# A decoder trunk on one core: the second MLP's down projection as seven block products in place of eight

## The chip, the core and the metric

The kernel runs on one core of one Trainium2 chip. The core has five engines that run side by side, each with its own queue in a fixed order: TensorE (PE; matrix products into PSUM), VectorE (DVE), ScalarE (ACT), GpSimd (POOL) and the queues that issue transfers (SP among them). The metric is the device time of one execution in microseconds, the median of several runs.

## What is computed

The reference is a decoder trunk of two layers on 1024 tokens of width 1024, all in fp32. The first layer mixes the tokens with a state-space recurrence, the second with stick-breaking attention. Each ends with a squared-ReLU MLP of inner width 4096:

```
h = modulate(rms_norm(x, mlp_norm_g[i]), sh_m, sc_m)
ff = einsum('bsf,fd->bsd', square(relu(einsum('bsd,df->bsf', h, mlp_w1[i]))), mlp_w2[i])
x = x + g_m[:, None, :] * ff
```

The change is in the second layer's `mlp_w2` product, 4096 x 1024 by 1024 tokens.

## The kernel before

Activations lie with features on the 128 partitions and tokens along the row, in tiles of 128 x 512: `xs[k][h]` is feature tile k (of 8) and token half h (of 2). Each fp32 product is made of three matmuls (`mm3`, lines 242 to 248): the weight and the activation are each split into a rounded upper part (written by ScalarE, type fp32r) and the rest (a subtraction on VectorE), and upper x upper, upper x lower and lower x upper are added in PSUM. A weight unit is 128 x 1024, eight blocks of 128 x 128; `load_unit` (line 205) fetches it into `raw`, and `split_unit` makes `uh` and `ul` of it. There are three buffers each of raw, uh and ul.

`mlp` (line 856) goes through the 32 inner tiles in eight groups of four. `up` makes one inner tile for one token half: 24 matmuls into a `pm` accumulator (two of these), relu on ScalarE, a square on VectorE (line 77), and the split of the result into two `f` tiles (ScalarE line 875, VectorE line 83). `down` takes the four inner tiles of a group to one output tile and token half: 12 matmuls into a `pa` accumulator (six of these), and one VectorE instruction, the gain (line 92): x = pa * mod + x. Group c's down part stands after the first up unit of group c + 1, so that TensorE has work while the last inner tiles are finished; then the other three up units of c + 1 follow. One w2 unit serves two output tiles; four make a group. The last group is different: its down part runs by token halves, and each finished tile is written out.

Outside the stretches that `keep_in_program_order` pins, a scheduler in the compiler sets the order of each queue; the MLP is such code. A tile's buffer is used again in turn, and the instruction that writes it next waits for all users of the old contents.

In the second MLP the norm's tiles (`acc`, `sq`, `rr`, `nt`) lie in a pool `np2` of their own, and `r` has two buffers, `f` 24.

## Time and profile before

| what | before |
|---|---|
| median of 3 runs | 2548.94 us (2546.42 to 2551.44) |
| the profiled execution | 2540.94 us, span 2539.2 us |
| TensorE busy | 2385.0 us, 94% of the span, 12704 matmuls |
| VectorE / ScalarE / GpSimd busy | 61% / 36% / 28% |
| mean granted TensorE clock | 0.975 of full speed |

The span is the time from the first to the last instruction; what lies around it is 1.7 us. In the profile a busy share over the whole span is a mean over stages: the second MLP fills roughly the last 700 us, and there GpSimd does nothing at all after its start. Matmuls overlap one another, so the listed time of one is longer than the distance from one to the next.

### The profile page before, as it was taken

What the parts mean: (1) busy time and instruction counts of PE and PEld (TensorE: products, weight loads), DVE (VectorE), ACT (ScalarE), POOL (GpSimd) and SP (SyncE); (2) the same over time, 40 slices, a digit from 0 to 9 for tenths busy, and PEclk for the clock granted to TensorE, in tenths of its full rate; (3) what the DMA queues carried; (4) which work ended last, traced back from release to release, by engine and by line L of the source; (5) the groups of instructions that cost most, each with busy time, mean ns of one, the idle gap of its engine ahead of it and who ended that gap; (6) DMA issues with size and microseconds to landing.
All of it is one profiled execution on the core that took longest, in us unless ns stands there. A gap on an engine that the chain in (4) does not pass through costs nothing.

```text
span 2539.2 us, 32956 instructions
## 1 busy us (share of the span) xinstructions
PE 2385.0 (94%) x12704; PEld 2009.2 (79%) x12704; DVE 1551.4 (61%) x2284; ACT 909.4 (36%) x1644; POOL 709.3 (28%) x795
## 2 busy tenths in 40 slices
PE   3888999999899999999899999999999999999999
PEld 2677788878687888888788888877788888888887
DVE  7997547776566553356777778788663333333334
ACT  4653124221121122133566666666341122112211
POOL 4664460385786000023333333332200000000000
PEclk8898999999999999999999999999999999999999
DMA  4325862767667441132111111246621111111112
GB/s 148 87 76 197 286 213 96 240 226 244 224 216 261 147 141 50 43 121 95 53 69 66 56 35 63 80 138 203 222 75 50 50 50 43 49 50 50 50 50 100
DMA packets 105918, 299.17 MB, mean 118 GB/s; under 512 B 13344, under 2 KB 25632, under 8 KB 105760
## 3 DMA queue, kind: packets, MB, share of 16 engines
q1 hardware_dynamic: 87840, 242.52, 28.1%
q0 software_dynamic: 15360, 50.34, 5.5%
q10 hardware_dynamic: 2560, 4.20, 0.7%
q8 instruction: 100, 1.64, 0.3%
q14 instruction: 58, 0.48, 0.1%
HBM read 243.33 MB, written 49.48 MB: 115 GB/s over the span
## 4 chain that ended last, share of the span: by engine, by line
PE 65%; DVE 15%; DMA 10%; issue 4%; ACT 2%; POOL 1%; SPq 0%; DVEq 0%; ACTq 0%; POOLq 0%
PE pm L69 8%; PE pm L246 8%; PE pm L247 8%; PE pm L248 8%; PE pa L248 6%; PE pa L246 6%; PE pa L247 6%; DMA raw<-in_adaT_dram 6%; PE pt L69 3%; DVE junk L173 3%; DVE sn L1114 3%; PE z L69 2%; PE po L69 2%; DMA raw<-in_wT_dram 1%; PE pv L246 1%
## 5 line engine op out<-in xcount | busy, mean ns | idle before, releaser
L246 PE MATMUL pm<-h,uh 128*128 128x512 f32 x1200 | 467.6, 392 | 7.6 <-ACT r L872 7.6
L248 PE MATMUL pm<-h,ul 128*128 128x512 f32 x1200 | 469.0, 391 | 4.5 <-DVE ul L83 4.4
L247 PE MATMUL pm<-h,uh 128*128 128x512 f32 x1200 | 468.8, 391 | 0.5 <-DVE h L92 0.5
L213 ACT CAST uh<-raw 128x1024 fp32r<-128x1024 f32 x162 | 170.4, 1052 | 741.9 <-PE pa L247 382.9
L246 PE MATMUL pa<-f,uh 128*128 128x512 f32 x848 | 332.1, 392 | 5.9 <-DVE xall L92 2.9
L247 PE MATMUL pa<-f,uh 128*128 128x512 f32 x848 | 331.7, 391 | 0.2 <-DVE f L83 0.2
L248 PE MATMUL pa<-f,ul 128*128 128x512 f32 x848 | 331.5, 391 | 0.0
L83 DVE TENSOR_TENSOR ul<-raw,uh 128x1024 fp32r<-128x1024 f32 x162 | 206.9, 1277 | 183.0 <-ACT uh L213 178.1
L246 PEld LDWEIGHTS pm<-h,uh 128*128 128x128 f32 x1200 | 225.9, 188 | 57.6 <-ACT r L872 10.6
L248 PEld LDWEIGHTS pm<-h,ul 128*128 128x128 f32 x1200 | 226.0, 188 | 52.7 <-DVE ul L83 5.8
L247 PEld LDWEIGHTS pm<-h,uh 128*128 128x128 f32 x1200 | 226.1, 188 | 47.5 <-DVE h L92 1.1
L92 DVE SCALAR_TENSOR_TENSOR x<-pa,mod,x 128x512 f32<-128x512 f32 x143 | 106.5, 750 | 204.6 <-PE pa L248 200.1
L173 DVE CUSTOM_DVE_ANT_0 junk<-raw,silr 128x1024 bf16<-128x1024 f32 x95 | 137.3, 1446 | 151.9 <-DMA raw<-in_adaT_dram 151.8
L69 PE MATMUL pm<-uh,h 128*128 128x256 f32 x960 | 225.4, 301 | 4.1 <-POOL h L74 3.0
L1114 DVE TENSOR_TENSOR_SCAN sn<-sn 128x768 f32<-128x768 f32 (+7 forms) x128 | 180.2, 1414 | 47.6 <-ACT sn L1109 46.3
L246 PEld LDWEIGHTS pa<-f,uh 128*128 128x128 f32 x848 | 160.0, 189 | 40.2 <-DVE xall L92 3.8
L247 PEld LDWEIGHTS pa<-f,uh 128*128 128x128 f32 x848 | 160.1, 189 | 33.7 <-DVE f L83 0.5
L248 PEld LDWEIGHTS pa<-f,ul 128*128 128x128 f32 x848 | 160.1, 189 | 33.2
L69 PEld LDWEIGHTS pm<-uh,h 128*128 128x128 f32 x960 | 170.3, 198 | 6.2 <-POOL h L74 3.2
L875 ACT CAST f<-r 128x512 fp32r<-128x512 f32 x128 | 79.5, 621 | 240.5 <-DVE r L77 240.5
L80 POOL TENSOR_TENSOR acc<-acc,sq 128x512 f32<-128x512 f32 x36 | 51.6, 1433 | 384.7 <-ACT sq L816 364.6
L77 DVE TENSOR_TENSOR r<-r 128x512 f32<-128x512 f32 (+1 forms) x130 | 97.5, 750 | 95.9 <-ACT r L872 95.9
(345 smaller groups left out, 4458.9 us busy)
## 6 DMA issues: line engine op xcount, KB each, us to landing
raw<-in_w_dram SPq DMA_DIRECT2D x144, 512.0 KB, 3.3
raw<-in_adaT_dram SPq DMA_DIRECT2D x96, 512.0 KB, 4.2
uh<-kh SPq DMA_DIRECT2D x40, 512.0 KB, 4.1
ul<-kl SPq DMA_DIRECT2D x40, 512.0 KB, 4.1
kh<-kr POOLq DMA_DIRECT2D x64, 256.0 KB, 2.6
kl<-ks POOLq DMA_DIRECT2D x64, 256.0 KB, 3.7
raw<-in_wT_dram SPq DMA_DIRECT2D x24, 512.0 KB, 4.2
raw<-in_wglu_dram SPq DMA_DIRECT2D x20, 512.0 KB, 4.4
```

Source lines behind the costliest of these rows:

```text
L69: return lambda *a, **k: tc.keep_in_program_order(f(*a, **k))
L77: eng.tensor_tensor(o, a, b, op=ALU.mult)
L80: eng.tensor_tensor(o, a, b, op=ALU.add)
L83: eng.tensor_tensor(o, a, b, op=ALU.subtract)
L92: V.scalar_tensor_tensor(o, a, s, b, op0=op0, op1=op1)
L173: V.tensor_tensor_reduce(junk, raw, row, 1.0, 0.0, op0=ALU.mult, op1=ALU.add, accum_out=bcol)
L213: ACT.copy(uh, raw)
L246: T.matmul(ps, uh[:, sl], hi, start=first, stop=False)
L247: T.matmul(ps, uh[:, sl], lo, start=False, stop=False)
L248: T.matmul(ps, ul[:, sl], hi, start=False, stop=last)
L875: ACT.copy(hi, r)
L1114: V.tensor_tensor_scan(g[:, s0:], g[:, s0:], g[:, s0:], 1.0, op0=ALU.mult, op1=ALU.bypass)
```

## The change

For groups 1 to 6 of the second MLP the down projection of one w2 unit is taken as a 2 x 2 block product. The left blocks are the weights: the two output tiles of the unit (i) by the inner tiles 0, 1 and 2, 3 (A11, A12, A21, A22, each two 128 x 128 blocks). The right blocks are the activations: the inner tiles 0, 1 and 2, 3 by the two token halves (B11, B12, B21, B22). Eight block products become seven, of block sums (Winograd's form): `RIGHT` says which right factor each takes. Products are 6 matmuls each, so an output pair is 42 in place of 48.

What that needs: per group, `enter` makes four sums of two tiles each (T1 to T4; eight VectorE instructions) and splits seven right blocks in place of four (14 tiles in place of 8). Per w2 unit, `blocks` copies the upper part of A11, A12 and A22 on ScalarE (768 wide) and makes the lower part on VectorE; then GpSimd makes four sums of 256 columns within raw and splits the result itself (a 1024-wide cast and a 1024-wide subtraction) into a second uh and ul. So a unit takes two of the three uh and ul buffers. Per output pair, the seven products end in seven gains and four adds on VectorE and one copy on ScalarE; the partial sums u and v are in the two `t` tiles, and three of the gains read those in place of PSUM.

Buffers in the second MLP: `r` six in place of two, `f` 30 in place of 24 (shared with the norm's tiles, which were in np2), `t` two, raw two in place of three. The pool is opened ahead of the output projection. w2's blocks are laid out in another order on the host (`W2_COLS`). Groups 0 and 7, and the first MLP, keep the plain form; in the last group two splits are made later (`plain`).

```diff
...
 LEAD = 24
+W2_COLS = (range(8), (0, 1, 2, 3, 6, 7, 4, 5))
...
     def open_x(i):
         es = ExitStack()
         pools["x"] = es.enter_context(tc.tile_pool(name=f"xp{i}", bufs=16 if i else 1))
-        pools["raw"] = es.enter_context(tc.tile_pool(name=f"raw{i}", bufs=3))
+        pools["raw"] = es.enter_context(tc.tile_pool(name=f"raw{i}", bufs=3 - i))
         es.callback(pools.pop, "raw")
         turns.clear()
         return es
...
             self.pool = (1, 3, 5, 7)
 
         def tile(self, tag, bufs):
+            if callable(self.np_):
+                return self.np_(tag, bufs)
             return self.np_.tile([P, HN], F32, tag=tag, name=nm(tag), bufs=bufs)
 
         def square(self, k, h):
...
                     stt(lo, t, shift, hi, ALU.add, ALU.subtract)
 
 
-    def mlp(layer, xs, hs, norm, mid=None, done=None):
+    def open_f(n):
+        fp = ctx_f.enter_context(tc.tile_pool(name="fp", bufs=1))
+
+        def ft(tag, bufs, dt=F32):
+            return fp.tile([P, HN], dt, tag=tag, name=nm(tag), bufs=bufs)
+
+        def f_tile(dt=F32R):
+            return ft("f", n, dt)
+
+        return ft, f_tile
+
+    def mlp(layer, xs, hs, norm, fs, mid=None, done=None):
         w1, w2 = A["w1"][layer], A["w2"][layer]
         gm = M_GM0 if layer == 0 else M_GM1
-        es = ExitStack()
-        fp = es.enter_context(tc.tile_pool(name="fp", bufs=1))
-
-        def ft(tag, bufs, dt=F32):
-            return fp.tile([P, HN], dt, tag=tag, name=nm(tag), bufs=bufs)
-
-        hid = {}
+        ft, f_tile = fs
+        hid, raws = {}, {}
 
         def up(f, u, h):
             p = ps_mm()
             for k in range(8):
                 mm3(p, u, k, hs[k][h], k == 0, k == 7)
-            r = ft("r", 2)
+            r = ft("r", 2 + 4 * layer)
             ACT.activation(r, p, AF.Relu)
             mul(r, r, r)
-            hi, lo = ft("f", 20 + 4 * layer, F32R), ft("f", 20 + 4 * layer, F32R)
+            return r
+
+        def halves(r):
+            hi, lo = f_tile(), f_tile()
             ACT.copy(hi, r)
             sub(lo, r, hi)
-            hid[f, h] = (hi, lo)
-
-        def down(c, o, u, j0, h):
+            return hi, lo
+
+        def down(c, o, u, i, h):
             p = ps_ax()
             for j in range(4):
-                mm3(p, u, j0 + j, hid[4 * c + j, h], j == 0, j == 3)
+                mm3(p, u, W2_COLS[layer][4 * i + j], hid[j, h], j == 0, j == 3)
             stt(xs[o][h], p, mod[:, gm + o:gm + o + 1], xs[o][h], ALU.mult, ALU.add)
+
+
+        def enter(j, h, r):
+            raws[j, h] = r
+            if h == 0 and j < 2:
+                hid["B11", j] = halves(r)
+            if (j, h) == (1, 1):
+                for i in range(2):
+                    t = ft("t", 2)
+                    sub(t, raws[i, 1], raws[i, 0])
+                    hid["T1", i] = halves(t)
+            if h == 1 and j >= 2:
+                i = j - 2
+                b11, b12, b21, b22 = raws[i, 0], raws[i, 1], raws[j, 0], raws[j, 1]
+                hid["B21", i] = halves(b21)
+                hid["B22", i] = halves(b22)
+                sub(b12, b22, b12)
+                hid["T3", i] = halves(b12)
+                add(b11, b11, b12)
+                hid["T2", i] = halves(b11)
+                sub(b21, b21, b11)
+                hid["T4", i] = halves(b21)
+
+        def blocks(c, op):
+            raw = raw_tile()
+            SP.dma_start(raw, w2[c, op])
+            h0, l0, h1, l1 = un_tile("uh"), un_tile("ul"), un_tile("uh"), un_tile("ul")
+            ACT.copy(h0[:, 0:768], raw[:, 0:768])
+            sub(l0[:, 0:768], raw[:, 0:768], h0[:, 0:768])
+            a11, a12, a22, a21 = [raw[:, 256 * n:256 * n + 256] for n in range(4)]
+            add(a22, a21, a22, G)
+            sub(a21, a11, a21, G)
+            sub(a11, a22, a11, G)
+            sub(a12, a12, a11, G)
+            G.tensor_copy(h1, raw)
+            sub(l1, raw, h1, G)
+            return {**{k: (h0, l0, 256 * n) for n, k in enumerate((1, 2, 4))},
+                    **{k: (h1, l1, 256 * n) for n, k in enumerate((6, 3, 5, 7))}}
+
+        RIGHT = {1: "B11", 2: "B21", 3: "B22", 4: "T4", 5: "T1", 6: "T2", 7: "T3"}
+
+        def seven(c):
+            us, sums, op_ = {}, {}, [0]
+
+            def gain(i, h, src):
+                k = 2 * op_[0] + i
+                stt(xs[k][h], src, mod[:, gm + k:gm + k + 1], xs[k][h], ALU.mult, ALU.add)
+
+            def product(op, n):
+                if op not in us:
+                    us[op] = blocks(c, op)
+                uh, ul, o = us[op][n]
+                p = ps_ax()
+                for i in range(2):
+                    hi, lo = hid[RIGHT[n], i]
+                    sl = slice(o + 128 * i, o + 128 * i + 128)
+                    T.matmul(p, uh[:, sl], hi, start=(i == 0), stop=False)
+                    T.matmul(p, uh[:, sl], lo, start=False, stop=False)
+                    T.matmul(p, ul[:, sl], hi, start=False, stop=(i == 1))
+                op_[0] = op
+                if n == 1:
+                    sums[op] = ft("t", 2), ft("t", 2)
+                    ACT.copy(sums[op][0], p)
+                if n < 3:
+                    gain(0, 0, p)
+                elif n == 4:
+                    gain(1, 0, p)
+                elif n == 6:
+                    add(sums[op][0], p, sums[op][0])
+                elif n == 5:
+                    u, v = sums[op]
+                    add(v, p, u)
+                    gain(0, 1, v)
+                elif n == 7:
+                    u, v = sums[op]
+                    add(u, p, u)
+                    gain(1, 0, u)
+                    add(v, p, v)
+                    gain(1, 1, v)
+                else:
+                    gain(0, 1, p)
+
+            for op in range(4):
+                for n in (1, 2, 4, 6, 5, 7, 3):
+                    product(op, n)
+
+        def plain(c, j, h, r):
+            raws[j, h] = r
+            late = c == 7 and layer == 1
+            if not late or h == 0 or j > 1:
+                hid[j, h] = halves(r)
+            elif j == 1:
+                hid[0, 1], hid[1, 1] = halves(raws[0, 1]), halves(r)
+
+        def fast(c):
+            return layer == 1 and 0 < c < 7
+
+        def ups(c, j):
+            u = load_unit(w1[4 * c + j])
+            for h in range(2):
+                r = up(4 * c + j, u, h)
+                if fast(c):
+                    enter(j, h, r)
+                else:
+                    plain(c, j, h, r)
 
         for h in range(2):
             for f in range(4):
                 u = load_unit(w1[f])
-                up(f, u, h)
+                plain(0, f, h, up(f, u, h))
                 if h == 0 and f == 0:
                     norm.rstd(1)
                 elif h == 0 and f == 1:
...
                     norm.apply(1, 0, 8)
         for c in range(8):
             if c < 7:
-                u = load_unit(w1[4 * c + 4])
-                up(4 * c + 4, u, 0)
-                up(4 * c + 4, u, 1)
-                for op in range(4):
-                    u = load_unit(w2[c, op])
-                    for i in range(2):
-                        for h in range(2):
-                            down(c, 2 * op + i, u, 4 * i, h)
-                    if mid is not None:
-                        mid()
-                for f in range(4 * c + 5, 4 * c + 8):
-                    u = load_unit(w1[f])
-                    up(f, u, 0)
-                    up(f, u, 1)
+                held = dict(hid)
+                hid.clear()
+                ups(c + 1, 0)
+                nxt = dict(hid)
+                hid.clear()
+                hid.update(held)
+                if fast(c):
+                    seven(c)
+                else:
+                    for op in range(4):
+                        u = load_unit(w2[c, op])
+                        for i in range(2):
+                            for h in range(2):
+                                down(c, 2 * op + i, u, i, h)
+                        if mid is not None:
+                            mid()
+                hid.clear()
+                hid.update(nxt)
+                for j in range(1, 4):
+                    ups(c + 1, j)
                     if mid is not None:
                         mid()
             else:
...
                     for op in range(4):
                         u = load_unit(w2[c, op])
                         for i in range(2):
-                            down(c, 2 * op + i, u, 4 * i, h)
+                            down(c, 2 * op + i, u, i, h)
                             done(2 * op + i, h)
-        es.close()
 
 
     def attention(xn, bias, xd):
...
         cyc[0] += 1
         pump((3, 4)[cyc[0] % 2])
 
-    mlp(0, xs, hs, norm=norm, mid=mid, done=done0)
+    ctx_f = ExitStack()
+    mlp(0, xs, hs, norm, open_f(20), mid=mid, done=done0)
+    ctx_f.close()
     norm1.rstd(1)
     norm1.spread(1)
     norm1.pool = (1, 4)
...
         for k in range(8):
             xs2[k][h] = xt()
             SP.dma_start(xs2[k][h], xd[k][h])
-    norm2.np_ = ctx.enter_context(tc.tile_pool(name="np2", bufs=1))
+    ctx_f = ctx
+    fs = open_f(30)
+    spare = {}
+
+    def norm_tile(tag, bufs):
+        n = spare.setdefault(tag, [0, []])
+        n[0] += 1
+        if len(n[1]) < bufs:
+            n[1].append(fs[1](F32))
+        return n[1][(n[0] - 1) % bufs]
+
+    norm2.np_ = norm_tile
 
     def oproj(i, h, mms):
         p = ps_mm() if (i, h) == (NONE, 1) else ps_ax()
...
     def done1(k, h):
         SP.dma_start(out[k][:, HN * h:HN * h + HN], xs2[k][h])
 
-    mlp(1, xs2, hs2, norm=norm2, done=done1)
+    mlp(1, xs2, hs2, norm2, fs, done=done1)
 
 
 def _constants(np):
...
     a["wo"] = unit(sb_w_o[0])
     a["wT"] = np.concatenate([w_kv.T, sb_w_q[0].T], 0).reshape(24, 128, 1024)
     a["w1"] = np.stack([unit(w) for w in mlp_w1])
-    a["w2"] = np.stack([w.reshape(8, 4, 128, 4, 2, 128).transpose(0, 3, 2, 4, 1, 5).reshape(8, 4, 128, 1024)
-                        for w in mlp_w2])
+    a["w2"] = np.stack([w.reshape(8, 4, 128, 4, 2, 128).transpose(0, 3, 2, 4, 1, 5).reshape(8, 4, 128, 8, 128)[
+        :, :, :, list(cols)].reshape(8, 4, 128, 1024) for w, cols in zip(mlp_w2, W2_COLS)])
     return {k: np.ascontiguousarray(v) for k, v in a.items()}
```

The queues differ as follows. On VectorE, a w2 unit within a group before: the second unit's split, then a gain for each output tile and token half, then the next unit's split (x are the output tiles, pa the accumulators).

```order
L83 TENSOR_TENSOR ul_18484<-raw_18481,uh_18483 128x1024
L92 SCALAR_TENSOR_TENSOR x_16428<-pa_18363,mod,x_16428 128x512
L92 SCALAR_TENSOR_TENSOR x_16444<-pa_18377,mod,x_16444 128x512
L92 SCALAR_TENSOR_TENSOR x_16430<-pa_18391,mod,x_16430 128x512
L92 SCALAR_TENSOR_TENSOR x_16446<-pa_18405,mod,x_16446 128x512
L83 TENSOR_TENSOR ul_18546<-raw_18543,uh_18545 128x1024
```

After, in the same place: the gains of one output pair, with the adds into u and v (t) between them, and behind them the short split (768 wide) for the unit of the pair after the next.

```order
L93 SCALAR_TENSOR_TENSOR x_16428<-pa_20345,mod,x_16428 128x512
L93 SCALAR_TENSOR_TENSOR x_16428<-pa_20356,mod,x_16428 128x512
L93 SCALAR_TENSOR_TENSOR x_16430<-pa_20364,mod,x_16430 128x512
L81 TENSOR_TENSOR t_20352<-pa_20372,t_20352 128x512
L81 TENSOR_TENSOR t_20353<-pa_20380,t_20352 128x512
L93 SCALAR_TENSOR_TENSOR x_16444<-t_20353,mod,x_16444 128x512
L81 TENSOR_TENSOR t_20352<-pa_20389,t_20352 128x512
L81 TENSOR_TENSOR t_20353<-pa_20389,t_20353 128x512
L93 SCALAR_TENSOR_TENSOR x_16444<-pa_20400,mod,x_16444 128x512
L93 SCALAR_TENSOR_TENSOR x_16430<-t_20352,mod,x_16430 128x512
L93 SCALAR_TENSOR_TENSOR x_16446<-t_20353,mod,x_16446 128x512
L84 TENSOR_TENSOR ul_20488<-raw_20485,uh_20487 128x768
```

So four instructions between two splits have become eleven; three of the gains take t as their input, and the short split stands behind all of them.

On TensorE before, the last product of one accumulator's chain and the beginning of the next; each chain of 12 is closed before the next begins.

```order
L248 MATMUL pa_18363<-f_18119,ul_18360 128x512
L246 MATMUL pa_18363<-f_18189,uh_18359 128x512
L247 MATMUL pa_18363<-f_18190,uh_18359 128x512
L248 MATMUL pa_18363<-f_18189,ul_18360 128x512
L246 MATMUL pa_18377<-f_17763,uh_18359 128x512
L247 MATMUL pa_18377<-f_17764,uh_18359 128x512
```

After, the end of the third product of a pair (from the first half-unit, uh_20333 and ul_20334) and what follows it, from GpSimd's half-unit (uh_20335 and ul_20336).

```order
L954 MATMUL pa_20364<-f_20184,ul_20334 128x512
L952 MATMUL pa_20372<-f_20094,uh_20335 128x512
L953 MATMUL pa_20372<-f_20095,uh_20335 128x512
L952 MATMUL pa_20380<-f_20008,uh_20335 128x512
L953 MATMUL pa_20380<-f_20009,uh_20335 128x512
L952 MATMUL pa_20389<-f_20089,uh_20335 128x512
L953 MATMUL pa_20389<-f_20090,uh_20335 128x512
L954 MATMUL pa_20372<-f_20094,ul_20336 128x512
L952 MATMUL pa_20372<-f_20179,uh_20335 128x512
L953 MATMUL pa_20372<-f_20180,uh_20335 128x512
L954 MATMUL pa_20372<-f_20179,ul_20336 128x512
L954 MATMUL pa_20380<-f_20008,ul_20336 128x512
```

The products 6, 5 and 7 are begun with their upper weights, two matmuls each, and only then does the first one come that needs GpSimd's lower part: 24 matmuls into the pair, where the upper part is needed after 18. Where a group's first pair stands, the products are not interleaved.

## Rows read from the trace of the kernel before

**Rows 1.** Busy time by stretch: time, busy us and count of each engine, clock, DMA.
```profile
core 0: us, PE busy (x) PEld busy (x) DVE busy (x) ACT busy (x) POOL busy (x), PEclk, DMA share, GB/s
420.00:800.00 380.00, 362.26 (x1576) 295.95 (x1574) 260.15 (x313) 83.19 (x117) 238.30 (x271) 0.98 0.66 227
1800.00:1850.00 50.00, 46.50 (x216) 37.48 (x215) 35.13 (x60) 22.34 (x33) 17.05 (x12) 1.00 0.51 192
1850.00:1900.00 50.00, 49.05 (x216) 40.29 (x215) 32.57 (x45) 22.49 (x33) 0.00 (x0) 1.00 0.28 92
1900.00:2500.00 600.00, 600.00 (x2648) 497.12 (x2647) 225.16 (x277) 121.95 (x164) 0.00 (x0) 1.00 0.15 50
```

**Rows 2.** The chain of waits from 1700 us to the end, by line.
```profile
by line: PE pa L248 14.3%; PE pa L246 14.2%; PE pa L247 14.2%; PE pm L246 13.7%; PE pm L247 13.7%; PE pm L248 13.7%; PE pm L69 3.7%; PE po L69 1.3%; PE z L69 1.1%; PE pt L69 1.0%; issue 0.9%; DMA ro<-od 0.9%; DMA ul<-kl 0.8%; DMA od<-o 0.8%
```

**Rows 3.** TensorE's waits from 1840 us to the end: total, times, longest.
```profile
PE pm L246 <- ACT r L872: 1.0, 1, 1.0
```

**Rows 4.** VectorE's timeline, second MLP, down projection: start us, us, what.
```profile
2004.26 0.75 DVE L92 SCALAR_TENSOR_TENSOR x<-pa,mod,x 128x512 f32<-128x512 f32 x1 [0.64 <-PE pa L248]
2006.98 0.75 DVE L92 SCALAR_TENSOR_TENSOR x<-pa,mod,x 128x512 f32<-128x512 f32 x1 [1.97 <-PE pa L248]
2009.70 0.75 DVE L92 SCALAR_TENSOR_TENSOR x<-pa,mod,x 128x512 f32<-128x512 f32 x1 [1.97 <-PE pa L248]
```

**Rows 5.** Groups of instructions, second MLP, 1900 to 2500 us: busy us, mean ns, idle before.
```profile
L92 DVE SCALAR_TENSOR_TENSOR x<-pa,mod,x 128x512 f32<-128x512 f32 x113 | 84.8, 750 | 168.6 <-PE pa L248 168.6
L83 DVE TENSOR_TENSOR ul<-raw,uh 128x1024 fp32r<-128x1024 f32 x56 | 68.6, 1226 | 106.0 <-ACT uh L213 103.0
L875 ACT CAST f<-r 128x512 fp32r<-128x512 f32 x54 | 33.5, 621 | 58.4 <-DVE r L77 58.4
L872 ACT ACTIVATE r<-pm 128x512 f32<-128x512 f32 x54 | 32.0, 593 | 75.2 <-PE pm L248 75.2
L246 PE MATMUL pa<-f,uh 128*128 128x512 f32 x451 | 175.6, 389 | 0.0
```

**Rows 6.** VectorE's timeline, a dense stretch of the first MLP.
```profile
433.36 0.69 DVE L83 TENSOR_TENSOR f<-r,f 128x512 fp32r<-128x512 f32 x1
433.96 0.75 DVE L92 SCALAR_TENSOR_TENSOR nt<-xall,scl,rr 128x512 f32<-128x512 f32 x1
434.62 1.22 DVE L83 TENSOR_TENSOR ul<-raw,uh 128x1024 fp32r<-128x1024 f32 x1
```

**Rows 7.** GpSimd's instructions by tile, whole run: ns shortest/median/longest.
```profile
L231 POOL CAST kr<-ks x64: 609/920/1656, 239.3 to 813.2; 128x512 fp32r<-128x512 f32 x64
L83 POOL TENSOR_TENSOR ks<-ks,kr x64: 1273/1302/2225, 240.0 to 813.8; 128x512 f32<-128x512 f32 x64
...
L69 POOL TENSOR_TENSOR vt<-k1m,k2m x16: 722/836/1639, 59.1 to 208.5; 128x256 f32<-128x256 f32 x16
...
L77 POOL TENSOR_TENSOR silr<-silr,row x1: 2350/2350/2350, 17.4 to 17.4; 128x1024 f32<-128x1024 f32 x1
```

**Rows 8.** Waits of the load queue after 1750 us; issues 1900 to 2500 us.
```profile
SPq L207 <- DVE ul L83: 653.4, 69, 11.0
...
raw<-in_w_dram SPq DMA_DIRECT2D x56, 512.0 KB, 3.2
```

**Rows 9.** VectorE beside GpSimd and without it, by tile or line; a GpSimd add.
```profile
L83 DVE TENSOR_TENSOR f<-r,f x34: 678/727/2200, 425.8 to 766.7; 128x512 fp32r<-128x512 f32 x34
...
L83 DVE TENSOR_TENSOR f<-r,f x54: 691/693/695, 1943.7 to 2495.4; 128x512 fp32r<-128x512 f32 x54
...
L92 DVE SCALAR_TENSOR_TENSOR nt<-x,scl,rr x16: 737/746/1629, 1829.2 to 1865.2; 128x512 f32<-128x512 f32 x16
...
L92 DVE SCALAR_TENSOR_TENSOR xall<-pa,mod,xall 128x512 f32<-128x512 f32 x40 | 29.2, 742 | 9.3 <-PE pa L248 9.2
...
L83 DVE TENSOR_TENSOR wt<-pt,wt x160: 525/674/693, 1221.2 to 1787.5; 128x512 fp32r<-128x512 f32 x96, 128x384 fp32r<-128x384 f32 x64
...
1828.02 2.23 POOL L80 TENSOR_TENSOR acc<-acc,sq 128x512 f32<-128x512 f32 x1 [0.74 <-ACT sq L816]
```

## The prediction

> **What bounds the kernel now.** I read first the table by stretch [rows 1]: from 1900 to 2500 us, inside the second MLP, TensorE is busy 600.00 of 600 us at a granted clock of 1.00 (the 2.4 GHz level), while VectorE works 225.16, ScalarE 121.95 and GpSimd nothing. The chain of waits from 1700 us on is led by six matmul lines, three of the up and three of the down projection, at about 14% each [rows 2]; so there TensorE sets the end. The list of TensorE's waits from 1840 us to the end holds one wait, 1.0 us [rows 3]. A matmul removed there is time removed, as long as nothing else becomes late.
>
> What one costs is its pitch, not its listed 389 ns: in the timeline of VectorE one gain follows the other after 2.72 us (2004.26, 2006.98, 2009.70), and each closes 12 matmuls, so 0.2267 us [rows 4]. A group's 384 matmuls (192 up, 192 down) take 87.0 us.
>
> **Removed: matmuls.** A down group goes from 4 x 2 x 2 x 12 = 192 to 4 x 7 x 6 = 168. Six groups: 6 x 24 = 144 matmuls, 144 x 0.2267 = 32.6 us. Weight loads go with them one for one. A group is then 360 matmuls, 81.6 us; one output pair (42 matmuls) takes 9.52 us, where it took 10.88.
>
> **VectorE.** Durations [rows 5, 9]: gain 0.75, 512-wide tensor_tensor 0.69, 1024-wide split 1.23, so a 768-wide one about 0.96 (estimate by the line through the last two). Per output pair it had four gains and a split, 4.2 us; now seven gains, four adds and the short split: 5.25 + 2.76 + 0.96 = 8.97 us of 9.52. In the up part it gains eight block sums and six splits, 9.7 us a group. Over a group that is 225.16/600 x 87.0 = 32.7 us before, plus 4 x 4.8 + 9.7 = 61.6 of 81.6 after: under TensorE, but in the products nearly level with it. Two things give it cover there. Durations overlap in the timeline: 0.60 to 0.67 us from start to start in a dense stretch [rows 6]. And six accumulators let it lag. In the order of the rows shown above the fifth product ends 32 matmuls, 7.25 us, into a pair; behind it VectorE has three adds, four gains and the split, 2.07 + 3.0 + 0.96 = 6.0 us, so it ends the pair at 13.3, some 3.7 us behind TensorE, and makes it up in the next pair before the fourth product comes: the sixth product's accumulator is free only when the pair before has done its gain of the seventh, so TensorE, which wants it 22 matmuls (5.0 us) into a pair, waits only once the lag passes about 6.7 us (5.0 plus the gain and the split that come behind). I cost this at nothing; without the overlap of durations it is the first thing to break.
>
> **ScalarE.** Six more fp32r copies at 0.62 us and four PSUM copies of the size of its 0.59 us relu [rows 5], less four times 0.2 us for the narrower weight copy: about 5 us more a group on an engine that is 20% busy [rows 1]. Its copy of the first product sits in front of that product's gain; it writes the buffer of u, which the pair before frees with its second last gain; VectorE then still has a gain and the short split, 1.7 us, beside which the copy runs. Nothing.
>
> **GpSimd** was idle; now it has, per output pair, four 256-wide sums, a 1024-wide cast and a 1024-wide subtraction. Nearest rows [rows 7]: 256-wide tensor_tensor 722 ns at best, 836 median, 1639 at most; 1024-wide 2350; the 512-wide subtraction 1273 at best, 1302 median, 2225 at most; the 512-wide cast 609, 920, 1656. No 1024-wide cast is in the trace: twice the median would be 1.8, twice the best 1.2, twice the longest 3.3. I take 0.73 (near the undisturbed end, because the stretch has few disturbing instructions), 1.4 and 2.4: X = 2.9 + 1.4 + 2.4 = 6.7 us a unit. The ends are 4 x 0.72 + 1.2 + 2.35 = 6.4 and 4 x 1.64 + 3.3 + 4.45 = 14.3.
>
> When must it be done? The first half-unit of a pair is copied when TensorE has left the pair before the last one (three slots of uh and ul, two taken per pair). For pair 1 that is the start of the products: ScalarE 0.84, VectorE 0.96, handovers 0.3, so GpSimd starts at 2.1 us. If it ran without a pause, the last half-unit of pair 3 would be ready at 2.1 + 3X; TensorE reaches its lower part at 3 x 9.52 + 24 x 0.2267 = 34.0 us. No stall while X is under 10.6 us. At 6.7 GpSimd pauses instead, for the short split: that is done 3.7 us into the pair before, the unit at about 10.5, and it is wanted at 9.52 + 5.44 = 15.0. Slack 4.5 us. GpSimd's 27 us a group of 81.6 are hidden.
>
> **Loads.** As many transfers as before, four a group, two raw buffers for three. Now each transfer waits for the split to free its buffer, 653.4 us in all, and lands 3.2 us after issue [rows 8]; so they are early, and one buffer less moves the issue, not the arrival. raw is now freed by GpSimd, about 1.5 us into the next pair; with 3.2 us of flight it lands at about 5 of 9.52. Cover 4.5 us.
>
> **The block sums between groups.** The last relu of a group is followed by eight VectorE instructions and the copies between them, about 10 us; the next group's first up unit (48 matmuls, 10.9 us) and two products (2.7) stand before the fourth block is wanted. Hidden, with some 3 us to spare.
>
> **The start of the MLP** (fp pool opened before the output projection, norm tiles out of f, third weight load behind the fetches): TensorE is idle 3.50 and 0.95 us in the two 50 us stretches there [rows 1], so it can gain 4.5 us at most, and I allow as much of a loss. Value 0.
>
> **The shared port.** In the first MLP, where GpSimd works 238.30 of 380 us [rows 1], VectorE's split of f (two SBUF inputs) has 678 / 727 / 2200 ns, against 691 / 693 / 695 where GpSimd is idle; the norm's instruction of the gain's kind, with two SBUF inputs, reaches 1629, right beside a GpSimd add of 2.23 us; but the gain with a PSUM input holds 742, and the PSUM split of wt at most 693 [rows 9]. So in a pair three gains (from t) and the split are exposed, the other eight instructions are not. The split finds GpSimd waiting for it. Of the three gains the last usually finds it idle; two meet the cast and the subtraction. A wait was at most 2200 - 693 = 1.5 us; half of it on average makes 8.97 + 1.5 = 10.5 us a pair, 0.95 over TensorE, and after three pairs a lag of 2.7 + 2.9 = 5.6 (2.7 is the 3.7 without the split), under 6.7. Cost 0, with 1 us taken for what comes through at group ends. GpSimd in its turn may be held by three gains, 2.3 us, inside its slack.
>
> The Trainium skill, "SBUF — State Buffer", section Who interferes with whom, says that whichever engine starts first keeps the pair for its whole instruction and the other blocks fully. By that a gain could wait for the whole wide subtraction rather than 1.5 us; the trace agrees that one is held back entirely, and has no wide subtraction on GpSimd to show how long. By the rule at its worst the sum would be the second figure of the first rival; by the rows, the forecast.
>
> **Sum.** -32.6 + 1 = -31.6 us. On the profiled execution, 2540.94 us with a span of 2539.2, that makes about 2509; it was 8 us quicker than the median of the runs shown, 2548.94. On that median: 2517 us.
>
> **Rivals.**
> 1. VectorE becomes the bound of the products through the port. For it: 8.97 of 9.52 us, and [rows 9]. Against: the overlap of durations, and GpSimd finishing before most gains from t. With the full 1.5 us twice a pair: 11.97, 2.45 over; after three pairs 2.7 + 7.4 = 10.1, 3.4 past the cover, six times 20 us: 2537. If two gains wait for a whole cast and subtraction, 1.4 + 2.4 us: 12.8, a lag of 12.4, 5.7 past the cover, 34 us: nothing is gained, 2550.
> 2. Slower: the half-units from GpSimd come late. Place: TensorE's first matmul with the lower half of the second half-unit. Price: 2.1 + 3X - 34.0 a group. From X = 12.4 us (5.4 a group, 32.6 in all) the kernel is slower; at the top of the rows, 14.3, it is 11 a group, 66 in all: 2582. For it: GpSimd's rows with VectorE beside it spread that far. Against: medians are near the minima, and the exposed VectorE instructions are few.
> 3. The change does what it says and the start of the MLP also moves: 2517 less or plus 4.5, inside the forecast's own range.
>
> **Chances.** Forecast with the third, 2512 to 2523: 0.66. First rival in part, 2523 to 2543: 0.19; in full, no change: 0.06. Second rival: 0.09. What a measurement can tell from no change is 0.2%, 5 us. So faster 0.85, same 0.06, slower 0.09. Range: from 2509 (all of the start's 4.5 us and 3 us of spread between runs) to 2538 (the first rival by the rows), which leaves out a little under 2 in 10.
>
> **What would show it.** After: 144 fewer matmuls into pa and TensorE full at clock 1.00 from 1900 us to the end; VectorE about 75% and GpSimd 33% busy there; GpSimd's unit near 6.7 us; gains from t longer on average than gains from pa. TensorE waiting for VectorE's x or t would mean the first rival; for GpSimd's ul, the second; for a transfer, that the two raw buffers are too few. I am wrong if TensorE's idle time in the second MLP exceeds 6 us.

## The result, and the profile after

The changed kernel takes 2510.1 us (2506.7 to 2519.8, 4 runs) where the kernel before took 2548.8 in the same sitting: a ratio of 0.986 [0.9843, 0.9877]. Run again it was 2517.5 us, 0.9883 [0.9862, 0.9904]. The forecast was 2517: the first median lies 7 us below it, and below the 2512 to 2523 that the prediction held likeliest; the second lies on it.

Most of what differs from run to run lies ahead of the change. What the change does is therefore read from a stretch: the matmuls that the program has from group 1's down projection on, counted back from the last one, from the start of the first to the start of the last. (It is a count, because the build issues one to four matmuls of that projection some 6 to 17 us early and others in their place.) In the profiles told of here this stretch starts anywhere from 1979.6 to 1997.8 us (2001.2 with fewer accumulators). Before it is 2448 matmuls in 554.65 us; after, 2304 in 522.01. The difference is 32.64 us, and 144 x 0.2267 is 32.64. In both profiles of the changed kernel the stretch is the same to 0.01 us, so what the two medians differ by, and the 6 us by which the first gain exceeds 32.64, is not the change's own; that the second median meets the forecast to a microsecond is in part luck.

The busy time by stretch, after (columns as in [rows 1]):

```profile
1800.00:1850.00 50.00, 46.10 (x210) 36.58 (x209) 35.24 (x59) 18.68 (x28) 15.95 (x12) 1.00 0.54 204
1850.00:1900.00 50.00, 48.94 (x219) 40.16 (x218) 33.53 (x46) 25.84 (x37) 0.00 (x0) 1.00 0.25 85
1900.00:2470.00 570.00, 570.00 (x2517) 472.12 (x2515) 411.96 (x532) 152.72 (x225) 169.99 (x144) 1.00 0.15 53
```

TensorE (first pair of numbers) is full at clock 1.00, as in [rows 1]. VectorE went to 72%, GpSimd from nothing to 30%, ScalarE to 27%, and none of it shows in TensorE. TensorE's waits from 1840 us to the end answer to [rows 3]: the same single one.

```profile
PE pm L247 <- ACT r L881: 1.0, 1, 1.0
```

The groups of instructions of the second MLP, 1900 to 2470 us (busy us, mean ns, idle before), answer to [rows 5] and show what was added:

```profile
L93 DVE SCALAR_TENSOR_TENSOR x<-pa,mod,x 128x512 f32<-128x512 f32 x114 | 82.3, 742 | 26.9 <-PE pa L249 24.9
L93 DVE SCALAR_TENSOR_TENSOR x<-t,mod,x 128x512 f32<-128x512 f32 x72 | 66.5, 944 | 0.8
L81 DVE TENSOR_TENSOR t<-pa,t 128x512 f32<-128x512 f32 x96 | 63.8, 684 | 21.2 <-PE pa L954 21.1
L84 POOL TENSOR_TENSOR ul<-raw,uh 128x1024 fp32r<-128x1024 f32 x24 | 63.5, 2646 | 1.9
L84 POOL TENSOR_TENSOR raw<-raw 128x256 f32<-128x256 f32 x72 | 59.2, 822 | 5.6
...
L930 POOL CAST uh<-raw 128x1024 fp32r<-128x1024 f32 x24 | 25.0, 1041 | 29.3 <-PE pm L248 28.2
L84 DVE TENSOR_TENSOR ul<-raw,uh 128x768 fp32r<-128x768 f32 x24 | 22.9, 953 | 29.5 <-ACT uh L923 29.5
L81 POOL TENSOR_TENSOR raw<-raw 128x256 f32<-128x256 f32 x24 | 22.3, 931 | 377.8 <-DVE ul L84 377.8
```

Gains from an accumulator take 742 ns, gains from t 944: two sorts, as the working had it. By tile (shortest, median, longest), again after:

```profile
L93 DVE SCALAR_TENSOR_TENSOR x<-pa,mod,x x114: 732/741/753, 1900.1 to 2468.2; 128x512 f32<-128x512 f32 x114
L93 DVE SCALAR_TENSOR_TENSOR x<-t,mod,x x72: 735/748/2105, 1991.5 to 2434.6; 128x512 f32<-128x512 f32 x72
```

The median is undisturbed; the longest stands beside GpSimd's subtraction. VectorE's timeline there (start us, us):

```profile
2073.12 2.10 DVE L93 SCALAR_TENSOR_TENSOR x<-t,mod,x 128x512 f32<-128x512 f32 x1
...
2083.10 1.09 DVE L93 SCALAR_TENSOR_TENSOR x<-t,mod,x 128x512 f32<-128x512 f32 x1
```

and GpSimd's:

```profile
2072.28 2.40 POOL L84 TENSOR_TENSOR ul<-raw,uh 128x1024 fp32r<-128x1024 f32 x1
...
2082.61 1.04 POOL L930 CAST uh<-raw 128x1024 fp32r<-128x1024 f32 x1
2083.73 2.74 POOL L84 TENSOR_TENSOR ul<-raw,uh 128x1024 fp32r<-128x1024 f32 x1
```

The first gain ends at 2075.22, 0.54 us after the subtraction (2074.68); the second at 2084.19, 0.54 after the cast (2083.65). So it is with each of the 30 gains from t, of 72, that start beside a GpSimd cast or subtraction: it ends 0.54 or 0.55 us after it. And the second subtraction, which starts while that gain runs, takes 2.74 where the free one took 2.40. The Trainium skill ("SBUF — State Buffer", Who interferes with whom) says that a VectorE instruction with two SBUF inputs and a GpSimd instruction that reads SBUF shut each other out for a whole instruction; these rows agree, in both directions.

### The profile page after: what moved, and what is told of

It is laid out like the page before. It is cut to its first block, busy times and chain, and to the rows that moved or that the text cites. A ratio compares the mean times of both kernels' runs of the same rounds, so it can differ in the third digit from the quotient of the medians.

```text
span 2510.7 us, 33266 instructions
## 1 busy us (share of the span) xinstructions
PE 2358.1 (94%) x12560; PEld 1986.0 (79%) x12560; DVE 1739.4 (69%) x2536; ACT 939.4 (37%) x1704; POOL 882.1 (35%) x939
## 4 chain that ended last, share of the span: by engine, by line
PE 65%; DVE 15%; DMA 10%; issue 4%; ACT 3%; POOL 1%; SPq 0%; DVEq 0%; ACTq 0%; POOLq 0%
PE pm L247 9%; PE pm L249 9%; PE pm L248 9%; PE pm L70 8%; DMA raw<-in_adaT_dram 5%; PE pa L953 3%; PE pa L952 3%; PE pa L954 3%; PE pa L247 3%; PE pa L249 3%; PE pa L248 3%; PE pt L70 3%; DVE sn L1236 3%; PE z L70 2%; PE po L70 2%
## 5 line engine op out<-in xcount | busy, mean ns | idle before, releaser
L214 ACT CAST uh<-raw 128x1024 fp32r<-128x1024 f32 x138 | 145.1, 1051 | 535.2 <-PE pa L248 155.1
L84 DVE TENSOR_TENSOR ul<-raw,uh 128x1024 fp32r<-128x1024 f32 (+1 forms) x162 | 202.5, 1250 | 141.2 <-ACT uh L214 109.4
L887 ACT CAST f<-r 128x512 fp32r<-128x512 f32 x152 | 94.3, 621 | 253.7 <-DVE r L78 216.7
L247 PE MATMUL pa<-f,uh 128*128 128x512 f32 x464 | 181.9, 392 | 3.3 <-DVE xall L93 2.7
L248 PE MATMUL pa<-f,uh 128*128 128x512 f32 x464 | 181.4, 391 | 0.2 <-DVE f L84 0.2
L249 PE MATMUL pa<-f,ul 128*128 128x512 f32 x464 | 181.1, 390 | 0.0
L81 POOL TENSOR_TENSOR acc<-acc,sq 128x512 f32<-128x512 f32 x24 | 34.7, 1445 | 351.8 <-ACT sq L819 351.7
L84 DVE TENSOR_TENSOR f<-r,f 128x512 fp32r<-128x512 f32 x152 | 124.4, 820 | 45.2 <-ACT f L887 43.9
L81 POOL TENSOR_TENSOR raw<-raw 128x256 f32<-128x256 f32 x24 | 22.3, 931 | 377.8 <-DVE ul L84 377.8
L70 PE MATMUL pm<-ul,h 128*128 128x256 f32 x480 | 138.4, 288 | 0.0
```

Source lines behind the costliest of these rows:

```text
L70: return lambda *a, **k: tc.keep_in_program_order(f(*a, **k))
L84: eng.tensor_tensor(o, a, b, op=ALU.subtract)
L214: ACT.copy(uh, raw)
L247: T.matmul(ps, uh[:, sl], hi, start=first, stop=False)
L248: T.matmul(ps, uh[:, sl], lo, start=False, stop=False)
L249: T.matmul(ps, ul[:, sl], hi, start=False, stop=last)
```

## The experiments

The stretch in us, from the profile of each (lost: above what as many matmuls take at the pitch of the kernel before, 0.22667), and the ratio to the kernel before. The kernels that add GpSimd work repeat instructions of the unit and leave nothing out.

| kernel | matmuls | stretch | lost | ratio [interval] |
|---|---|---|---|---|
| before | 2448 | 554.65 | 0 | 1 |
| changed | 2304 | 522.01 | 0 | 0.986, 0.9883 |
| e1 groups plain | 2448 | 554.65 | 0 | 0.9988 [0.9974, 1.0002] |
| e2 three groups | 2376 | 538.33 | 0 | 0.9945 [0.9926, 0.9964] |
| e4 no GpSimd | 2304 | 522.01 | 0 | 0.9871 [0.9833, 0.9909] |
| e6 four accumulators | 2304 | 523.11 | 1.1 | 0.9893 [0.9852, 0.9934] |
| e10 one cast more | 2304 | 565.28 | 43.3 | 1.0019 [1.0, 1.0038] |
| e3 one subtraction more | 2304 | 555.43 | 33.4 | 1.0009 [0.999, 1.0028] |
| e7 the same, gains from PSUM | 2304 | 531.55 | 9.5 | 0.9923 [0.9909, 0.9938] |
| e8 three casts more | 2304 | 623.70 | 101.7 | 1.0298 [1.0283, 1.0313] |
| e3 long | 2304 | 656.64 | 134.6 | 1.0402 [1.0357, 1.0446] |
| e5 last group too | 2280 | 519.43 | 2.9 | 0.9856 [0.9835, 0.9878] |
| e9 last group, gains from PSUM | 2280 | 521.22 | 4.6 | 0.9859 [0.9843, 0.9875] |

**Is it the matmuls?** Three kernels: the changed one again, one whose `fast` returns False, so that all eight groups are plain and all else stays, and one with three groups.

```
-            return layer == 1 and 0 < c < 7
+            return False                             # e1_plain
+            return layer == 1 and c in (1, 3, 5)     # e2_half
```

> The changed kernel once more, for a narrower figure. Theory A (TensorE alone sets the end; the gain is 144 matmul pitches of 0.2267 us): 32.6 us under the kernel before, a ratio of 0.9872. Theory B (the other buffers, the earlier pool and the reordered start of the MLP bring something of their own, as the first median of 38.7 us suggests): 36 to 40 us under it, 0.984 to 0.986.

> The changed kernel with all groups in the plain form of eight products: the new pools, buffer counts, norm tiles and weight layout stay, the seven products go. Theory A: the time of the kernel before within the noise, at most 4.5 us to either side (the idle time at the start of the MLP). Theory B: 4 to 6 us faster than before.

> Seven products in three of the six groups (1, 3 and 5). Theory A: half the gain, 3 x 24 x 0.2267 = 16.3 us over the changed kernel and 16.3 under the one before. Theory B: about 20 us under the kernel before, since its part does not depend on the number of groups.

Without the products 2545.7 us against 2550.0; by the ratio 3 us less, by its interval between 6.6 less and 0.5 more. The rest of the change is thus worth nothing that can be told from 0 or from a few us; its stretch is that of before to 0.01 us. With three groups 2533.6, 16.5 less by the medians, and the stretch shorter by 16.32, which is 72 x 0.2267. The gain is proportional to the matmuls removed.

**Does VectorE nearly bound it?** In e4 VectorE does GpSimd's sums and subtraction too, and ScalarE the cast; in e6 the pool of accumulators holds four instead of six.

```
-            add(a22, a21, a22, G)          # and the three sums after it
+            add(a22, a21, a22)
-            G.tensor_copy(h1, raw)
-            sub(l1, raw, h1, G)
+            ACT.copy(h1, raw)
+            sub(l1, raw, h1)
```

```
-        pools["ax"] = es.enter_context(tc.tile_pool(name=f"pax{i}", bufs=4 if "pv" in pools else 6, space=PSUM))
+        pools["ax"] = es.enter_context(tc.tile_pool(name=f"pax{i}", bufs=4, space=PSUM))
```

> GpSimd's work goes elsewhere: the cast to ScalarE, the four sums and the subtraction to VectorE; GpSimd is idle and its port free. VectorE has 8.97 + 4 x 0.42 + 1.23 = 11.9 us of listed time per output pair of 9.52 us. If listed durations count, the lag after three pairs is 2.7 + 7.1 = 9.8 us, 3.1 past the cover, 19 us in all over the changed kernel. If the overlap of about 0.08 us for each of 16 instructions counts, 10.6 us a pair, a lag of 5.9 and no more than 5 us over it. The chain from the arrival of a unit to its last half is on one engine then, so TensorE may also wait for ul.

> Four accumulators for the down projection in place of six, in every stage that has the pool open. If VectorE really ends each pair 3 us or more behind TensorE, TensorE must now wait for x in the products: 1 us or more a pair, 24 pairs, 20 us and more over the changed kernel. If the lag is smaller than worked out, under 5 us.

Neither costs what the times can tell from nothing; e6's stretch is 1.1 us longer. The stretch from 1900 to 2450 us of e4:

```profile
1900.00:2450.00 550.00, 550.00 (x2428) 455.40 (x2428) 416.37 (x640) 169.35 (x240) 0.00 (x0) 1.00 0.16 52
```

VectorE now has four sums of 0.413 us and a split of 1.22 more in each pair, 11.8 us of listed durations, and TensorE is still full. VectorE's timeline at the first gains of the second pair of a group and of the third, with no idle time between:

```profile
2083.16 1.40 DVE L93 SCALAR_TENSOR_TENSOR x<-pa,mod,x 128x512 f32<-128x512 f32 x2
2093.51 1.40 DVE L93 SCALAR_TENSOR_TENSOR x<-pa,mod,x 128x512 f32<-128x512 f32 x2
```

A pair takes it 10.35 us: less than the listed durations, by the overlap of [rows 6] (the expectation's second figure was 10.6), and still 0.83 more than TensorE's 9.52. VectorE falls behind inside a group, and the accumulators take that up: the closest that one comes is to be read out 2.3 us before TensorE writes it again. e6 is a weaker test than its expectation says: with four accumulators the build puts all products in sequence, so the order of TensorE changed with their number. There the closest is 0.06 us, once in each group. In e4 the gains from t have no GpSimd beside them: 737/741/747.

**Does GpSimd have 4 us to spare?** The prediction says that a unit may take 10.6 us. In the changed kernel it takes 7.1 (the first of a group 13.1, in the up part), and GpSimd idles 2.2 us between the third unit and the fourth. The first two kernels repeat the subtraction (e3_mid), and that twice with one cast more (e3_long).

```
             sub(l1, raw, h1, G)
+            sub(l1, raw, h1, G)            # e3_mid
```

> GpSimd makes the lower half-unit twice over (one more 1024-wide subtraction of the same data), so a unit takes 7.1 + 2.65 = 9.8 us in place of 7.1. By the bound of the prediction (2.1 + 3X - 34.0 us a group, no stall under X = 10.6) nothing changes but the port waits: at most 5 us over the changed kernel, TensorE without a wait for ul. Rival (GpSimd's work is already on the path, or VectorE breaks through the port): 10 us or more over it, with waits of TensorE for x, t or ul.

> GpSimd makes the cast twice and the lower half-unit three times: X = 7.1 + 1.04 + 2 x 2.65 = 13.4 us. By the bound 2.1 + 40.2 - 34.0 = 8.3 us a group, 50 us in all: about 2560, slower than the kernel before, and TensorE waits for GpSimd's ul and uh. Rival (the three buffers of uh and ul hold more in hand than the bound says): under 25 us over the changed kernel.

Both forecasts failed, and of e3_mid the rival (10 us or more) came true: the doubled subtraction takes the whole gain away. TensorE's waits of e3_mid from 1840 us on:

```profile
PE pa L953 <- DVE x L93: 16.2, 12, 1.5
PE pm L249 <- DVE ul L84: 2.3, 6, 0.4
```

TensorE does not wait for GpSimd, as the second rival has it, but for VectorE's gains, as the first has it. And gains from t are held longer there:

```profile
L93 DVE SCALAR_TENSOR_TENSOR x<-t,mod,x x69: 735/828/2842, 1992.1 to 2456.8; 128x512 f32<-128x512 f32 x69
```

In e3_long, at 13.4 us a unit, TensorE does wait for GpSimd too: 20.8 us for its halves beside 26.1 for gains.

That gave two theories, P (the port holds gains, VectorE comes late) and L (the length of the unit, 9.8 us and more, against the 9.52 of a pair). e7 keeps the doubled subtraction and lets all gains read PSUM: the sums are written into the accumulators of the fifth and seventh products, and ScalarE makes the one SBUF copy still needed. e8 lengthens the unit by casts instead.

```
...
-                    add(v, p, u)
-                    gain(0, 1, v)
+                    add(p, p, u)
+                    ACT.copy(v, p)
+                    gain(0, 1, p)
+                    p5[op] = p
...
-                    add(u, p, u)
-                    gain(1, 0, u)
-                    add(v, p, v)
-                    gain(1, 1, v)
+                    add(p5[op], p, v)
+                    add(p, p, u)
+                    gain(1, 0, p)
+                    gain(1, 1, p5[op])
```

```
             G.tensor_copy(h1, raw)
+            G.tensor_copy(h1, raw)         # e10: once; e8: three times
```

> The doubled subtraction of e3_mid stays, but the three gains that read t now read PSUM: the sums are added into the accumulators of the fifth and seventh products, and ScalarE makes the one copy in SBUF that is still needed. Measure: first matmul of group 1's down projection to the last matmul, 522.0 us in the changed kernel, 555.4 with the doubled subtraction. Theory P (two-input gains from SBUF wait for the wide subtraction, VectorE comes late, TensorE waits for accumulators): the gains are no longer exposed, only the short split is, so 522 to 528 us, and about 0.987 to 0.990 of the time before. Theory L (what counts is the length of GpSimd's unit, 9.8 us and more of 9.52 a pair, whoever waits for it): nothing changes, 550 to 560 us, ratio 0.999 to 1.003.

> The changed kernel with GpSimd's wide cast written four times in place of once; gains from t as in the changed kernel. GpSimd's unit grows by 3 x 1.12 us to 10.5 us, longer than with the doubled subtraction (9.8). Theory P: a gain beside a cast took 752 to 769 ns in the trace with the long unit, so a cast holds nothing back; the one subtraction moves 3.4 us later and meets more gains, each waiting 1.4 us at most as in the changed kernel. 522 to 530 us, ratio 0.987 to 0.990. Theory L: at least what the doubled subtraction cost, 555 us or more, ratio 1.000 or more.

e7 loses 9.5 us where e3_mid lost 33.4, with a unit of the same length: the length alone does not make three quarters of the loss, and e7 is 3.5 us beyond theory P's range. That the gains' inputs made the difference is not shown: TensorE's order differs between the two as well, in the way that e10 below tells of. TensorE's waits of e7 from 1840 us on:

```profile
PE pm L249 <- DVE ul L84: 2.4, 6, 0.4
PE pa L953 <- DVE x L93: 1.6, 6, 0.3
```

e8 missed P by 94 us, but P had a false premise: four gains of 752 to 769 ns beside a cast had only met its last 0.2 us. Here one meets more of it. VectorE, then GpSimd, in e8:

```profile
2101.95 1.09 DVE L93 SCALAR_TENSOR_TENSOR x<-t,mod,x 128x512 f32<-128x512 f32 x1
```

```profile
2101.46 1.04 POOL L931 CAST uh<-raw 128x1024 fp32r<-128x1024 f32 x1
2102.57 1.38 POOL L932 CAST uh<-raw 128x1024 fp32r<-128x1024 f32 x1
```

The gain ends at 2103.04, 0.54 us after the cast (2102.50), and the next cast takes 1.38. A cast holds the port like a subtraction, so e8 lengthened the unit and the hold at once and tells the two theories apart no more.

**One cast.** The smallest step, 1.1 us more a unit, with a third theory: the short split that lets GpSimd begin stands on VectorE behind gains that wait for GpSimd, a loop.

> The changed kernel with GpSimd's wide cast written twice, so that a unit grows from 7.1 to 8.2 us; nothing else. Measure: first matmul of group 1's down projection to the last matmul, 522.0 us in the changed kernel. Slack theory (the prediction's: a unit may take 10.6 us): 522.0, ratio 0.986 to 0.990. Loop theory: the short split that lets GpSimd begin its next unit stands on VectorE behind gains that wait for the subtraction of the unit before, so a unit's period is its length plus VectorE's 2.2 us between (9.26 us in the changed kernel, under the 9.52 us of a pair; with a doubled subtraction 12.8, with four casts 14.4). Then the period becomes 10.4 us at the least and 11.8 if a gain is caught, the shortest of GpSimd's pauses inside a group stays at 2 us or more instead of closing to 1.1, and TensorE loses 1 to 4 us a group: 528 to 546, ratio 0.989 to 0.997.

It cost 43.3 us, more than the subtraction of 2.4 us, and every theory missed. TensorE's waits of e10 from 1840 us on:

```profile
PE pa L953 <- DVE x L93: 13.1, 12, 1.3
PE pa L953 <- DVE t L81: 6.5, 6, 1.1
PE pm L249 <- DVE ul L84: 3.0, 4, 1.8
```

GpSimd's timeline shows that it is not the bound: between the last three units of a group it now idles 4.4 and 6.0 us, where it was 4.7 and 2.2 in the changed kernel, and its halves are ready some 2.6 us or more before TensorE reads them.

```profile
2082.34 2.76 POOL L84 TENSOR_TENSOR ul<-raw,uh 128x1024 fp32r<-128x1024 f32 x1
2089.48 0.74 POOL L81 TENSOR_TENSOR raw<-raw 128x256 f32<-128x256 f32 x1 [4.38 <-issue]
...
2094.95 2.40 POOL L84 TENSOR_TENSOR ul<-raw,uh 128x1024 fp32r<-128x1024 f32 x1
2103.40 0.73 POOL L81 TENSOR_TENSOR raw<-raw 128x256 f32<-128x256 f32 x1 [6.04 <-issue]
```

What did change is TensorE's program. The build orders each engine's instructions, and with a longer GpSimd unit it puts the matmuls with the lower half of the unit's weights later. For pairs 2 and 3 of a group (numbers are products, "first" their first two matmuls, "rest" the other four):

```
changed:  1 2 4 | 6 5 7 first | 6 5 7 rest | 3 | 1' 2' 4' | 6' 5' 7' first ...
e10:      1 2 4 | 6 5 7 3 first | 1' 2' | 6 5 7 3 rest | 4' | 6' 5' 7' 3' first ...
```

In the changed kernel 26 matmuls, 5.9 us, stand between the end of product 7 and the fifth product of the next pair, which takes over its accumulator; in e10 it is 12, 2.7 us. In that time VectorE has to read product 7 out. Its timeline there:

```profile
2093.59 0.69 DVE L81 TENSOR_TENSOR t<-pa,t 128x512 f32<-128x512 f32 x1 [3.58 <-PE pa L955]
2094.49 0.69 DVE L81 TENSOR_TENSOR t<-pa,t 128x512 f32<-128x512 f32 x1 [0.22 <-PE pa L955]
2095.22 2.68 DVE L93 SCALAR_TENSOR_TENSOR x<-t,mod,x 128x512 f32<-128x512 f32 x1
2097.83 1.27 DVE L81 TENSOR_TENSOR t<-pa,t 128x512 f32<-128x512 f32 x2
...
2101.01 1.40 DVE L93 SCALAR_TENSOR_TENSOR x<-pa,mod,x 128x512 f32<-128x512 f32 x2
```

The gain from t is held from 2095.22 to 2097.90 by the subtraction that ends at 2097.35; the adds that read product 7 come behind it, until 2099.10; TensorE, which wanted that accumulator at 2097.9, goes on at 2099.16. Without the hold of 1.94 us the adds would be done by 2097.2; in the changed kernel's order the accumulator would be wanted 3.2 us later. Either alone would leave no wait at this place. The next wait is the dearer one (the line of 13.1 us above, against 6.5):

```profile
2101.80 0.80 PE L953 MATMUL pa<-f,uh 128*128 128x512 f32 x1 [1.25 <-DVE x L93]
```

It is product 3 of the new pair, now opened right behind product 7. It takes over the accumulator of product 1 of the same pair, which VectorE, late by then, reads out from 2101.01 to 2101.75; in the changed kernel's order 12 more matmuls, 2.7 us, stand ahead of it. All this is worked out from these rows, not shown by a run: the hold of the port and the order of TensorE were not separated, since every kernel with a longer unit got such an order in at least one pair of a group, e7 in the last one too. The next run would have been one cast more with four accumulators, where the build has nothing to run ahead with (e6 has all products in sequence); it was not tried.

Part of the loss is the clock. Two stretches of e10, behind those waits:

```profile
2095.00:2100.00 5.00, 3.93 (x17) 2.71 (x16) 4.96 (x6) 0.84 (x1) 2.36 (x1) 1.00 0.31 106
2100.00:2105.00 5.00, 3.75 (x10) 2.61 (x10) 3.93 (x6) 0.59 (x1) 1.46 (x2) 0.66 0.01 4
```

After waits of 1.24 and 1.42 us the granted clock falls to 0.66 on average, so part of the second of these is at the 1.2 GHz level, and matmuls start 0.43 us apart for about 2.5 us. Of e10's 43.3 us, 28.4 are gaps of over 0.5 us and 14.9 are matmuls at a slower pitch. Of these 14.9, 8.8 fall where the granted clock was at the lower level; the other 6.1 are matmuls just behind a wait, most of them 0.32 to 0.34 us apart, at the full clock. So about a fifth of the loss is pitch at the lower clock; e7 lost its 9.5 us without leaving the 2.4 GHz level.

**Is there a faster version?** e5 does the last group in seven products too, and writes each output when its last sum is in; e9 does that with gains from PSUM, and in the last pair takes products 6, 5 and 7 before 2, 4 and 3, so that one gain follows the last matmul.

```
-            return layer == 1 and 0 < c < 7
+            return layer == 1 and 0 < c              # e5, e9
+            elif fast(c):                            # at c == 7
+                seven(c)
...
-                for n in (1, 2, 4, 6, 5, 7, 3):      # e9
+                for n in (1, 6, 5, 7, 2, 4, 3) if (c, op) == (7, 3) else (1, 2, 4, 6, 5, 7, 3):
```

> The seventh group in the seven-product form as well, each output written as soon as its last sum is in; its four weight units are then loaded once in place of twice. Theory A: 24 matmuls fewer, 5.4 us, less what VectorE still has to do behind the last product (four instructions in place of one, about 2.1 us): 3.3 us under the changed kernel. Rival: the sixteen output transfers come closer together at the end and take it back: no change or up to 3 us slower.

> Gains from PSUM as in e7 without the extra subtraction, the last group too in seven products, and in its last output pair the products of the sums before the other three, so that one gain follows the last matmul. 12536 matmuls. From the first matmul of group 1's down projection to the end of the span: 527.0 us in the changed kernel (522.0 and 5.0 behind the last matmul), 525.8 with the last group in seven products as before (519.4 and 6.4). 24 matmuls less are 5.4 us; if the lateness of VectorE in the last group caused its 2.8 us of waits and the 1.4 us more at the end, 521.5 to 523. If the waits come from the block sums at the start of the last group, 524 to 526. Ratio 0.984 to 0.987 either way: the trace decides, not the medians.

e5 is 6 us quicker than the changed kernel beside it by the medians, with overlapping intervals, but its profiled stretch began 12.0 us earlier, in code that is the same. What its own part gives is 5.44 us of matmuls, less 2.85 lost in the last group, less 1.46 more behind the start of the last matmul (6.39 for 4.93), where adds and gains wait for the last products: 1.1 us. TensorE's waits in its last 110 us:

```profile
PE pa L954 <- DVE t L81: 1.0, 1, 1.0
PE pa L954 <- DVE x L93: 0.7, 1, 0.7
```

e9 lost 4.6 us there and has 7.9 us behind the start of the last matmul, so it is 2.1 us longer than the changed kernel over the same code; its expectation failed. No version here beats the changed kernel by more than can be told.

## Why the prediction was right, point by point

- **Removed matmuls, 32.6 us.** Measured 32.64, and 16.32 with half the groups; that TensorE stays full is what decided the result. The 1 us taken for leftovers was not needed. The sum on the profiled execution gave 2509; the profiled run after took 2512.5, of which 4.2 us arose before the stretch.
- **VectorE "nearly level".** Hidden, as forecast. The 8.97 us of 9.52 are listed durations, and the overlap that the prediction names but does not take off is real: in e4 11.8 us listed took 10.35. VectorE was 72% busy where 75% was worked out.
- **Six accumulators as cover, lag 3.7 of 6.7 us.** Right in size. The gains of product 3 that close the first and the second pair of a group, and TensorE's first matmul into their accumulators again:

```profile
2077.01 0.74 DVE L93 SCALAR_TENSOR_TENSOR x<-pa,mod,x 128x512 f32<-128x512 f32 x1
2079.90 0.39 PE L952 MATMUL pa<-f,uh 128*128 128x512 f32 x1
...
2085.31 0.74 DVE L93 SCALAR_TENSOR_TENSOR x<-pa,mod,x 128x512 f32<-128x512 f32 x1
2089.42 0.39 PE L952 MATMUL pa<-f,uh 128*128 128x512 f32 x1
```

  They are free 2.15 and 3.37 us ahead, where 3.0 were worked out, and nowhere in the seven products is it less than 2.15. VectorE's short split ends 4.4 and 4.1 us behind TensorE's pair, where the lag was to be 3.7; the cover is larger too, by the second gain that stands behind this one in most pairs and that the prediction did not count. So this margin is real but not wide.
- **GpSimd's unit, X = 6.7 us.** It takes 7.1: by the means 3.4 for the four sums (2.9 taken), 1.04 for the cast (1.4) and 2.65 for the subtraction (2.4). No stall, as forecast; the third unit of a group is ready 3.4 us before TensorE reads its lower half (2086.47, 2089.88), the least of all, where 4.5 were worked out.
- **"No stall while X is under 10.6 us", and the second rival from X = 12.4.** This step is wrong. At 8.2 us the gain is already gone (e10, 1.0019), by waits for VectorE and not for late half-units. The step kept TensorE's order fixed while X grew; the build changes it with X.
- **The port, a wait of at most 1.5 us.** In the changed kernel the longest was 2105 - 748 = 1.36 us, and the mean over 72 gains 0.2, or 0.6 a pair where 1.5 were taken. But the bound was an accident of which instructions the kernel before had: with two subtractions in a row a gain took 2842 ns, 2.1 us too long. That a gain waits for the whole instruction, put down as the dearer figure of the first rival, is what the rows bear out; the first rival's mechanism is there, and in the changed kernel its price is 0.
- **ScalarE, the loads, the block sums between groups.** TensorE waits for none of them. The load queue's waits for a free buffer after, 1900 to 2470 us, answer to [rows 8]:

```profile
SPq L921 <- DVE ul L84: 195.1, 24, 10.5
SPq L208 <- DVE ul L84: 138.2, 31, 10.9
SPq L921 <- POOL ul L84: 122.2, 12, 13.2
SPq L208 <- POOL ul L84: 86.0, 12, 7.2
```

  raw is freed by GpSimd in part, as worked out, and still early enough.
- **The start of the MLP.** TensorE idles 3.90 and 1.06 us in the two stretches of 50 us, where it was 3.50 and 0.95; e1, which has this part alone, is 3 us quicker than before by the ratio, with an interval from 6.6 quicker to 0.5 slower. That agrees with the value 0; the interval reaches beyond the 4.5 us allowed.

## What to carry to other kernels

On a full TensorE, fewer matmuls pay at their pitch to the last hundredth, as long as what replaces them stays off its path; measure that from the first to the last matmul of the stretch, where the spread of the rest of the program does not enter. A slack that is worked out from the order of one build holds for that build alone: one cast of 1.04 us more a unit, on an engine that is 30% busy, came with another order of TensorE and cost 43 us, so look at the new order before trusting such a slack. Give GpSimd work that reads SBUF only where VectorE, at the time, reads at most one of its inputs from there.

## What was not expected of the hardware

- Held instructions follow one pattern: a gain with two SBUF inputs that starts beside a GpSimd cast or subtraction ends 0.54 or 0.55 us after it (all 30 in the changed kernel), and a GpSimd instruction that starts beside such a gain takes some 0.3 us longer (1.04 to 1.38 in e8, 2.40 to between 2.72 and 2.74 in the changed kernel).
- GpSimd's 1024-wide fp32r cast takes 1.04 us, less than half of the two-input subtraction of that width (2.40).
- VectorE's 256-wide sum takes 0.413 us where GpSimd's takes 0.73 undisturbed, and adds into PSUM cost the same as into SBUF (697 for 684 ns in e7 and in the changed kernel).
- After two waits of 1.24 and 1.42 us in a stream that is otherwise full, matmuls started 0.43 us apart for about 2.5 us at a mean granted clock of 0.66: 8.8 us of e10's 43.3 are the slower pitch at the lower clock, beyond the waits themselves.
